# A tile of 64 bytes given up in a transformer layer on one core: the pools behind it begin 64 bytes lower

## The chip, the core and the metric

The kernel runs on one core of a Trainium2 chip. The metric is the device time of one execution in microseconds (us). TensorE (PE in the profile) multiplies: a matmul streams one operand from the on-chip memory SBUF against weights that a separate instruction (LDWEIGHTS, engine PEld) has loaded from SBUF. VectorE (DVE), ScalarE (ACT) and GpSimd (POOL) do the element-wise work, and SyncE (SP) and POOL issue the DMAs. SBUF has 128 partitions; an address below is a byte offset within a partition.

## What is computed

One layer of a bidirectional encoder, 1024 tokens by 1024 channels, in float32. Cut to what matters:

```python
mod = silu(c) @ w_ada + b_ada                 # sh1, sc1, gt1, sh2, sc2, gt2
h = rmsnorm(x, norm1_g) * (1 + sc1) + sh1
u, v, q, k, va, gate_a, gate_b = split(h @ w_in)
a_out = gmlp_branch(u, v, ...) @ w_a          # chunks of 128 positions
b_out = window_attention_branch(q, k, va, ...) @ w_b   # |t-s| <= 128, ALiBi, sink
merged = sigmoid(gate_a) * a_out + sigmoid(gate_b) * b_out
x = x + gt1 * (merged @ w_o)
h2 = rmsnorm(x, norm2_g) * (1 + sc2) + sh2
f_gate, f_up = split(h2 @ w_ffn_in)           # 2816 columns each
x = x + gt2 * ((silu(f_gate) * f_up) @ w_ffn_out)
```

## The kernel before

**Precision.** Each float32 operand is split into a high part rounded to the fast matmul type and a low rest (`A.copy` and a subtraction on DVE: `unit` L223, `split` L411, `split2` L1254). A product of two operands is three matmuls: high by high, high by low, low by high (`mm3` L231, `multiply` L1378). So the matmuls come in triples.

**Stages.** `half(0)` and `half(1)` (L643, called at L1780) do the input projection, the gMLP branch and the attention for 512 tokens each, up to about 390 us. `gate_products` (L1387) does the gates' projection and the merge for the remaining channels, `out_products` (L1491) the output projection, the second norm and the first steps of what follows. Then comes the feed-forward input projection with 22 column tiles (L2049 to L2123), from about 590 us, and the down projection (L2125 to L2250), from about 1014 us. From the gate products on, each 2x2 block product is done with seven block products instead of eight, after Strassen and Winograd: the list `STEPS` (L1374) names for each of the seven the weight unit, the streamed block and the PSUM bank. A step of the feed-forward (one column tile) is therefore 7 products of 12 matmuls with 512 columns: 4 row blocks by one triple. The order in a step is B11, B21, T2, T1, T3, B22, T4. The blocks B11 and B21 are tiles `h`; T3 and T4 are tiles of the pool mid; T1, T2 and B22 are tiles `tt1`, `tt2`, `b22` of the pool ffn (`fpt` L1248; the names in the profile are those of the tile, so a block T2 of the feed-forward appears as `b22h`, `b22l` and its B22 as `tt2h`, `tt2l`, L1792 and L1972). The weights are tiles `wh` and `wl`. Two weight units of the feed-forward lie in the ffn tile `first` (L1676). In the down projection (77 steps of 12 matmuls) `split_step` (L2040) puts three of five units into `wh` and `wl` and two of five into tiles `oh` and `ol` of the pool outp; there each unit holds both the weights and the streamed block.

**Order of the work.** In `out_products` a planner (`Plan`, L41) sorts the work of the engines by cost and due time; behind it the order is written out by hand. TensorE runs its queue in program order, and loads of units are issued one step and more ahead of their use.

**Where the tiles lie.** The pools are laid out one behind another: const, wpool, hpool, mid, t2, small (L156 to L161), and behind small whatever is open: apool and attp during `half` (L323), then ffn (`open_ffn` L573), then outp (L2126). Each buffer takes a multiple of 32 bytes. In the program before, the places are these:

| Pool | first tile at byte | remainder by 256 |
|---|---|---|
| const (`ident`, `zeros`, `identr`) | 16512 | 128 |
| wpool (`raw`, `wh`, `wl`) | 19776 | 64 |
| hpool (`h`) | 56640 | 64 |
| mid | 89408 | 64 |
| small | 171328 | 64 |
| `ngt1` in small | 175296 | 192 |
| `ngt` in small, 4 buffers | 175360 | 0 |
| apool, later ffn, later outp | 175488 | 128 |
| attp (`pt`, `vt`, `lb`) | 198848 | 192 |

All tiles of wpool, hpool, mid, ffn and outp have sizes that are multiples of 2048, so every one of them has the remainder of its pool. `kbuf` in apool is at 188608, remainder 192.

**The tile of the change.** `out_products` needs the gate of the output projection negated: eight numbers per partition, written once (L1501) and used as the scalar of `accumulate` (L1607) for the products whose sign is turned. Before, it is the tile `ngt1` of 16 numbers with one buffer. The down projection has a tile with the same use for four numbers of the second gate, `sm(4, "ngt")` (L2191), written at L2235 and read in `second_row` (L2184); `sm` (L193) makes a tile of pool small with the pool's four buffers.

Of the kernel before, what the change touches and what calls it, by code (L numbers as in the profile page):

```python
# [8 lines left out]
F32 = mybir.dt.float32  # L9
# [7 lines left out]
P = 128  # L17
D = 1024
S = 1024
KT = D // P  # L20
# [87 lines left out]
def kernel(  # L108
# [52 lines left out]
    small = ctx.enter_context(pool("small", 4))  # L161
# [5 lines left out]
    def nm(s):  # L167
        n_names[0] += 1
        return f"{s}_{n_names[0]}"
# [13 lines left out]
    def midt(dt, shape):  # L183
        return mid.tile([P, 2048], dt, tag="mid", name=nm("mid")).rearrange(
            "p (a b) -> p a b", a=shape
        )
# [6 lines left out]
    def sm(n, name):  # L193
        return small.tile([P, n], F32, tag=name, name=nm(name))
# [1296 lines left out]
    def out_products(merged):  # L1491
# [5 lines left out]
        B22 = oblk["B22"] = (fpt("b22h"), fpt("b22l"))  # L1497
        T3 = oblk["T3"] = (midt(F32R, 4), midt(F32R, 4))
        T4 = oblk["T4"] = (midt(F32R, 4), midt(F32R, 4))
        ngt = small.tile([P, 16], F32, tag="ngt1", name="ngt1", bufs=1)  # L1500
        V.tensor_scalar(ngt[:, :KT], mod[:, GT1 : GT1 + KT], -1.0, None, op0=ALU.mult)  # L1501
        gt = mod[:, GT1 : GT1 + KT]

# [280 lines left out]
    with tc.manual_schedule():  # L1784
        out_products(merged)
# [263 lines left out]
    with tc.manual_schedule():  # L2049
# [141 lines left out]
        ngt = sm(4, "ngt")  # L2191
# [130 lines left out]
```

## Time and profile before

| | us |
|---|---|
| median of 3 runs | 1229.14 (1228.86 to 1229.53) |
| the profiled execution, its time | 1231.04 |
| its span, first to last instruction | 1229.2 |
| TensorE busy in the span | 1217.7 |
| VectorE busy | 928.8 |
| ScalarE busy | 582.5 |

A row of a group of instructions gives the line (L145 is the helper that records every instruction, so tiles tell more than lines), engine, operation, the tiles as out<-in, shape, count, and then busy time and mean duration, or minimum/median/maximum. Matmuls overlap: the next one starts before the modelled end of the one before, so the distance between starts is the cost of one, and a longer duration shows a longer distance. In the chain of waits in order of time a row is start, length, what ran, and how many instructions; matmuls that end in one `mm` or `at` bank group stand in one row.

### The profile page before, as it was taken

What the parts mean: (1) busy time and instruction counts of PE and PEld (TensorE: products, weight loads), DVE (VectorE), ACT (ScalarE), POOL (GpSimd) and SP (SyncE); (2) the same over time, 40 slices, a digit from 0 to 9 for tenths busy, and PEclk for the clock granted to TensorE, in tenths of its full rate; (3) what the DMA queues carried; (4) which work ended last, traced back from release to release, by engine and by line L of the source; (5) the groups of instructions that cost most, each with busy time, mean ns of one, the idle gap of its engine ahead of it and who ended that gap; (6) DMA issues with size and microseconds to landing.
All of it is one profiled execution on the core that took longest, in us unless ns stands there. A gap on an engine that the chain in (4) does not pass through costs nothing.

```text
span 1229.2 us, 15626 instructions
## 1 busy us (share of the span) xinstructions
PE 1217.7 (99%) x5653; PEld 1007.4 (82%) x5653; DVE 928.8 (76%) x1504; ACT 582.5 (47%) x954; POOL 150.8 (12%) x182
## 2 busy tenths in 40 slices
PE   9999999999999999999999999999999999999998
PEld 7888888888788888878778888888888888888887
DVE  8999977789978776898897667575676766765646
ACT  5667855367855543645453333333333334433341
POOL 0024323024322000011000001010000000000001
PEclk9999999999999999999999999999999999999999
DMA  9743169644277333467313446455555449995552
GB/s 362 275 184 100 35 225 357 240 183 160 104 257 239 97 120 103 145 231 240 130 42 121 171 156 221 171 189 187 188 188 191 167 153 369 394 352 189 188 171 103
DMA packets 78097, 236.54 MB, mean 192 GB/s; under 512 B 8899, under 2 KB 9155, under 8 KB 72773
## 3 DMA queue, kind: packets, MB, share of 16 engines
q1 hardware_dynamic: 63028, 163.20, 38.3%
q0 software_dynamic: 14992, 72.36, 15.6%
q8 instruction: 44, 0.72, 0.2%
q14 instruction: 33, 0.26, 0.1%
HBM read 176.28 MB, written 59.24 MB: 192 GB/s over the span
## 4 chain that ended last, share of the span: by engine, by line
PE 92%; DVE 4%; DMA 2%; ACT 1%; issue 1%; SPq 0%; DVEq 0%; ACTq 0%
PE at L145 47%; PE mm L145 46%; DVE mid L145 1%; DMA raw<-in_w_q_dram 1%; DMA raw<-in_w_ada_dram 1%; DVE wl L145 1%; DVE t L145 0%; DMA mid<-in_xA_dram 0%; DVE wo L145 0%; DVE raw L145 0%; DVE pL L145 0%; ACT wh L145 0%; ACT mid L145 0%; DVE ss L145 0%; DVE tt1l L145 0%
## 5 line engine op out<-in xcount | busy, mean ns | idle before, releaser
L145 ACT CAST wh<-raw 128x1024 fp32r<-128x1024 f32 (+1 forms) x149 | 152.0, 1022 | 112.0 <-PE mm L145 33.4
L145 DVE TENSOR_TENSOR wl<-raw,wh 128x1024 fp32r<-128x1024 f32 (+1 forms) x135 | 158.9, 1181 | 60.4 <-ACT wh L145 59.9
L145 PE MATMUL mm<-mid,wh 128*128 128x512 f32 x640 | 198.9, 392 | 0.8 <-DVE mid L145 0.8
L145 PEld LDWEIGHTS mm<-mid,wh 128*128 128x128 f32 x640 | 119.8, 188 | 26.9 <-DVE mid L145 1.2
L145 PE MATMUL mm<-mid,wl 128*128 128x512 f32 x320 | 125.3, 392 | 0.0
L145 PE MATMUL mm<-wh,h 128*128 128x512 f32 x384 | 124.7, 396 | 0.6 <-ACT h L145 0.6
L145 PE MATMUL at<-h,wh 128*128 128x512 f32 x304 | 94.1, 391 | 0.8 <-DVE t L145 0.8
L145 PE MATMUL mm<-h,wh 128*128 128x512 f32 x304 | 94.3, 391 | 0.0
L145 PEld LDWEIGHTS mm<-wh,h 128*128 128x128 f32 x384 | 70.8, 188 | 14.1 <-ACT h L145 1.0
L145 DVE TENSOR_TENSOR wl<-ws,wh 128x1024 fp32r<-128x1024 f32 (+1 forms) x54 | 60.7, 1124 | 24.8 <-ACT wh L145 24.7
L145 ACT CAST wh<-ws 128x1024 fp32r<-128x1024 f32 (+1 forms) x54 | 52.6, 973 | 43.8 <-DVE ws L145 35.6
L145 PEld LDWEIGHTS mm<-mid,wl 128*128 128x128 f32 x320 | 60.0, 188 | 13.7
L145 PE MATMUL mm<-wl,h 128*128 128x512 f32 x192 | 71.1, 391 | 0.0
L145 PEld LDWEIGHTS at<-h,wh 128*128 128x128 f32 x304 | 56.8, 188 | 13.2 <-DVE t L145 1.6
L145 PEld LDWEIGHTS mm<-h,wh 128*128 128x128 f32 x304 | 56.7, 188 | 11.6
L145 ACT ACTIVATE t<-t 128x512 f32<-128x512 f32 x46 | 28.4, 630 | 71.6 <-DVE t L145 71.5
L145 DVE TENSOR_TENSOR ol<-raw,oh 128x1024 fp32r<-128x1024 f32 x30 | 36.6, 1224 | 31.9 <-ACT oh L145 30.4
L145 PE MATMUL mm<-h,wl 128*128 128x512 f32 x152 | 59.3, 390 | 0.0
L145 PE MATMUL at<-h,wl 128*128 128x512 f32 x152 | 59.2, 389 | 0.0
L145 ACT ACTIVATE xs<-xs 128x512 f32<-128x512 f32 x21 | 13.3, 632 | 96.2 <-DVE xs L145 96.2
L145 ACT CAST oh<-raw 128x1024 fp32r<-128x1024 f32 x30 | 31.6, 1054 | 45.3 <-PE at L145 23.6
L145 PE MATMUL at<-wl,wh 128*128 128x512 f32 (+1 forms) x136 | 52.8, 388 | 0.0
(296 smaller groups left out, 2885.7 us busy)
## 6 DMA issues: line engine op xcount, KB each, us to landing
mid<-in_w_ada_dram SPq DMA_DIRECT2D x28, 512.0 KB, 8.6
raw<-in_w_gate_dram SPq DMA_DIRECT2D x28, 512.0 KB, 3.8
tA<-hid POOLq DMA_DIRECT2D x11, 1024.0 KB, 4.3
tB<-hid POOLq DMA_DIRECT2D x11, 1024.0 KB, 5.0
wo<-in_w_out_dram POOLq DMA_DIRECT2D x22, 512.0 KB, 6.1
wS<-wo POOLq DMA_DIRECT2D x11, 1024.0 KB, 5.3
raw<-wS SPq DMA_DIRECT2D x44, 256.0 KB, 3.2
raw<-tB SPq DMA_DIRECT2D x44, 256.0 KB, 5.2
```

The costliest lines, as they stand in the source:

```text
L145: ins = f(*args, **kw)
```

## The change

The negated gate becomes a tile of the tag `ngt`, which has four buffers already. The tag's buffers are 32 bytes each afterwards (eight numbers); before, 16 bytes that took 32. The tile `ngt1` of 64 bytes is gone, so what lies behind pool small begins at 175424 instead of 175488. No instruction is added or removed.

```diff
-        ngt = small.tile([P, 16], F32, tag="ngt1", name="ngt1", bufs=1)
+        ngt = sm(KT, "ngt")
         V.tensor_scalar(ngt[:, :KT], mod[:, GT1 : GT1 + KT], -1.0, None, op0=ALU.mult)
         gt = mod[:, GT1 : GT1 + KT]
```

## Prediction

> **What bounds the kernel.** I read the page first, then the chain of waits in order of time, then the matmul groups by tile, then the timeline inside one feed-forward step.
>
> ```profile
> span 1229.2 us, 15626 instructions
> PE 1217.7 (99%) x5653; PEld 1007.4 (82%) x5653; DVE 928.8 (76%) x1504; ACT 582.5 (47%) x954; POOL 150.8 (12%) x182
> PE 92%; DVE 4%; DMA 2%; ACT 1%; issue 1%; SPq 0%; DVEq 0%; ACTq 0%
> ```
>
> TensorE is busy for 99% of the span, and 92% of the chain that ends last is TensorE. A change that adds and removes no instruction can only show if it changes what one matmul costs, or how often TensorE starves. The table by stretches says that starving is not the question behind 640 us:
>
> ```profile
> core 0: us, PE busy (x) PEld busy (x) DVE busy (x) ACT busy (x) POOL busy (x), PEclk, DMA share, GB/s
> 640.00:1020.00 380.00, 380.00 (x1658) 310.89 (x1657) 259.39 (x359) 130.05 (x178) 29.34 (x55) 1.00 0.49 174
> ```
>
> The clock granted is 1.00, DVE is busy for 259 of 380 us, and 1658 matmuls fill the 380 us: 229.2 ns from start to start. Is that what a 512-column matmul costs here? The chain in order of time (start, length, what, how many) says no:
>
> ```profile
> 153.00 5.44 PE mm L145 x24
> ...
> 347.22 46.27 PE mm L145 x204
> 407.25 5.49 PE mm L145 x24
> 426.50 5.49 PE mm L145 x24
> ...
> 534.55 30.40 PE mm L145 x132
> ...
> 569.86 16.49 PE mm L145 x72
> ...
> 706.59 38.51 PE at L145 x168
> ...
> 1014.74 60.05 PE at L145 x264
> 1074.79 60.09 PE mm L145 x264
> ```
>
> Where it goes best, 24 matmuls take 5.44 us (226.7 ns each), and 204 in a row keep that (46.27 / 204 = 226.8). Elsewhere, with no wait shown, the same shape takes 229.2 (38.51 / 168) and 227.5 (60.05 / 264). Which matmuls are the dear ones? By tile (duration min/median/max; the modelled end lies after the next start, so only differences count: 389 belongs to a spacing of 227, 394 to 232):
>
> ```profile
> L145 PE MATMUL at<-h,wh x304: 387/389/497, 393.3 to 1000.3; 128*128 128x512 f32 x152
> L145 PE MATMUL mm<-h,first x24: 390/395/398, 611.3 to 619.7; 128*128 128x512 f32 x24
> L145 PE MATMUL at<-h,first x24: 392/395/504, 614.2 to 623.3; 128*128 128x512 f32 x24
> ```
> ```profile
> L145 PE MATMUL at<-tt1h,wh x112: 388/394/478, 398.8 to 1005.6; 128*128 128x512 f32 x112
> L145 PE MATMUL at<-tt1h,wl x112: 392/392/397, 399.3 to 1006.0; 128*128 128x512 f32 x112
> L145 PE MATMUL at<-tt1l,wh x112: 387/388/397, 399.0 to 1005.8; 128*128 128x512 f32 x112
> ```
>
> The products that stream `h` are at the floor. Those that stream `tt1` (a tile of the pool ffn) are 394, 392, 388 in each triple of three: 5 + 3 - 1 = 7 ns over three floors of 389. `first` is `h` against weights in the same pool, and costs 6 more. The timeline of one step shows it in starts:
>
> ```profile
> 764.28 0.61 PE L145 MATMUL mm<-h,wh 128*128 128x512 f32 x2
> ...
> 769.73 0.40 PE L145 MATMUL mm<-b22h,wh 128*128 128x512 f32 x1
> ...
> 775.24 0.40 PE L145 MATMUL mm<-mid,wh 128*128 128x512 f32 x1
> ```
>
> Two products (24 matmuls) on `h` take 769.73 - 764.28 = 5.45 us, two on `b22` and `tt1` take 5.51. What the dear tiles have in common is where they lie. Added up from the pools in the code, the tiles of wpool, hpool and mid all start 64 bytes above a multiple of 256, and those of ffn and outp, behind the 4160 bytes of pool small, 128 above one. The dear matmuls are those in which the streamed tile and the weights differ in this (`tt1`, `tt2`, `b22` against `wh`; `h` against `first`), and about a dozen behind each change from one to the other: the 24 of 407.25 and 426.50 are a product on mid right behind one on ffn and one on `h`, 0.05 us above 5.44.
>
> **The change, part by part.** It adds and removes no instruction. The rows of the tile `ngt`:
>
> ```profile
> L145 DVE SCALAR_TENSOR_TENSOR mid<-mm,ngt,mid x12: 737/749/751, 538.8 to 580.9; 128x512 f32<-128x512 f32 x12
> L145 DVE SCALAR_TENSOR_TENSOR mid<-mid,ngt,mid x8: 743/746/747, 1208.2 to 1215.6; 128x512 f32<-128x512 f32 x8
> L145 DVE TENSOR_SCALAR ngt<-mod x2: 169/170/172, 143.2 to 1091.0; 128x8 f32<-128x8 f32 x1, 128x4 f32<-128x4 f32 x1
> ```
>
> (1) **The slot.** The gate is written once (0.17 us) and read twelve times until 580.9; the other `ngt` is written at 1091.0. The tag has four buffers for these two tiles, so no wait arises: 0. If the second had to wait for the first's readers, it would wait for something that ended 510 us earlier: still 0.
>
> (2) **The address.** ngt1 took 64 bytes. The tag ngt had four buffers of 16 bytes, each in a 32-byte slot, and has four of 32 now: 0 more. Pool small shrinks from 4160 to 4096 bytes, and apool, attp, ffn and outp begin 64 lower, so ffn and outp go from 128 to 64 above a multiple of 256, like all other matmul tiles from the gate products on; attp goes from 192 to 128. With a floor of 226.7 the terms are:
> - Feed-forward: a step has 7 products, 84 matmuls. 38.51 us for 168 is 0.43 above 168 x 0.2267 = 38.08, 0.21 for a step; 22 steps give 4.7.
> - Gate products: the starts 407.25 and 426.50 are 84 matmuls apart, 19.25 against 19.04: 0.21, six times: 1.3.
> - Output projection: 30.40 - 132 x 0.2267 = 0.48 and 16.49 - 72 x 0.2267 = 0.17: 0.65.
> - `first`: 48 matmuls by 395 - 389 = 6 ns: 0.3.
> - Down projection, where two of five weight units lie in outp: 264 matmuls are 59.85 at the floor and take 60.05 and 60.09, 0.22 above; 924 matmuls give 3.5 times this, 0.8.
>
> The sum is 7.7. All of it lies on the path, as TensorE has no idle time there. A little will stay (behind the row sums and spreads, which work on tiles of const, and at the stage borders): I take 7.4.
>
> (3) **Attention**, the first 385 us, is not cleaned: there attp goes from 192 to 128 while its partners stay at 64, and the tiles of const at 128.
>
> ```profile
> L145 PE MATMUL at<-kbuf,mid x128: 274/337/409, 78.9 to 321.3; 128*128 128x384 f32 x96, 128*128 128x256 f32 x32
> ```
>
> No row shows these tiles at 128. The bounds: 128 score products and, by the code, 88 products with `vt` (22 key blocks, two heads, two parts), 216 in all, each getting dearer by 9 ns (the widest step from median to maximum in the `tt1` rows, 388 to 397) is +1.9; each getting cheaper by the 5 ns of `tt1h` against `h` is -1.1. Score products stay between unlike tiles, as now, so I take 0 and keep both ends.
>
> (4) **Other engines.** The subtractions into a tile at 64 and into one at 128:
>
> ```profile
> L145 DVE TENSOR_TENSOR wl<-raw,wh 128x1024 fp32r<-128x1024 f32 x125 | 152.1, 1220 | 54.4 <-ACT wh L145 53.9
> ...
> L145 DVE TENSOR_TENSOR ol<-raw,oh 128x1024 fp32r<-128x1024 f32 x30 | 36.6, 1224 | 31.9 <-ACT oh L145 30.4
> ```
>
> 1220 and 1224 ns: DVE doesn't tell the places apart, 0. DMAs of equal size into the two places land so:
>
> ```profile
> ws<-in_w_up_dram SPq DMA_DIRECT2D x11, 512.0 KB, 5.7
> ru<-in_w_up_dram SPq DMA_DIRECT2D x11, 512.0 KB, 3.5
> ```
>
> `ru` moves to the residue of `ws`. At worst its loads take 2.2 us longer; by the code each is issued over one step (19.25 us between the starts 407.25 and 426.50) ahead of its use, and what it could delay is DVE, idle for 120 of those 380 us. I take 0.
>
> So 1229.14 - 7.4 = **1221.7**. The durations are those of the profiled execution, 1231.04 us with a span of 1229.2; it is 0.15% above the median, and the term is small enough to subtract it from the median as it is.
>
> **The rivals.** (a) *No difference, 1229.1.* The dear matmuls are dear for what they do, not for where they lie: all `tt` and `b22` products follow an eviction, or stream blocks just made. For it: no view shows an address. Against it: `first` holds weights, not a streamed block, and is dear too, while products on `h` with the same loop are at the floor. That the shift doesn't happen (a slot of 16 bytes that really grew to 32) ends here too. The Trainium skill, page "SBUF — State Buffer", section "Who interferes with whom", gives TensorE two independent read ports for streamed operand and weights and says "PE and ACT never wait on anyone"; by that rule the place of a tile can't matter and the time is this rival's. The trace disagrees so far: equal shapes, no wait, 389 against 394.
>
> (b) *Half.* Only the steady part goes (by the code 3 products of 12 matmuls in 22 + 6 + 4 steps, 1152 on ffn tiles, by 7/3 = 2.3 ns: 2.7 us, and the 0.3 of `first`), since transitions have another cause: 1229.14 - 3.0 = 1226.1. Against it: the transitions sit only behind ffn and outp tiles.
>
> (c) *Slower, by collision.* If streamed tile and weights hurt each other when they start on the same residue, all products on ffn now do so all the time. The price: every matmul on an ffn tile at the maximum of the `tt1` rows, 397, is 8 above the floor instead of 7/3, so 5.7 more in 1152: +6.5, 1235.6. It decides for slower as soon as equal residues cost more than those 2.3 ns. Against it: `h` and `wh` are at equal residues and at the floor.
>
> **How the numbers follow.** The forecast gets 0.78; its own range is 7.7 + 1.1 better, 1220.3, to 7.4 less 1.9, 1223.6. (b) gets 0.06, (a) 0.11, (c) 0.05. From 1220.0 to 1226.5 the range holds the forecast and (b), a little over 8 in 10. About 0.2% (2.5 us, so below 1226.7) is what a measurement of this kernel can tell from no change: faster 0.84, same 0.11, slower 0.05.
>
> **What would show it.** Right: 168 chained feed-forward matmuls in 38.1 us instead of 38.51; medians of `tt1h`, `b22h` and `first` at 389; the span of the first 385 us within 2 us. Wrong: `tt1h` still at 394 (a), mid products behind it still 0.05 above (b), `tt1` rows at 397 (c), or TensorE waits that weren't there, were something else nearly late.

## The result and the profile after

| | before | after |
|---|---|---|
| median, first comparison (5 runs each) | 1228.86 us (1227.65 to 1229.53) | 1223.76 us (1222.79 to 1225.07) |
| its ratio | | 0.9959 [0.9945, 0.9974] |
| median, later comparison (11 and 5 runs) | 1230.84 us (1228.22 to 1231.62) | 1223.26 us (1220.81 to 1224.36) |
| its ratio | | 0.9940 [0.9928, 0.9952] |
| span of the profiled execution of the first | 1229.2 us | 1223.2 us |

Faster, by 5.1 us in the first comparison and 7.6 in the later one, both ratios with their intervals below 1; 7.4 were forecast. Page of the kernel after: span, busy times, engines' shares of the chain of waits.

```profile
span 1223.2 us, 15626 instructions
PE 1212.0 (99%) x5653; PEld 1008.0 (82%) x5653; DVE 928.0 (76%) x1504; ACT 583.1 (48%) x954; POOL 150.6 (12%) x182
PE 94%; DVE 4%; issue 1%; DMA 1%; ACT 1%; SPq 0%; DVEq 0%; ACTq 0%
```

Nothing was taken out: the same 15626 instructions, the same 5653 matmuls, DVE, ACT and POOL as before within a us. TensorE alone is busy for 5.7 us less and is still the bound. The stretch from 640 to 1020 us (same columns as before):

```profile
640.00:1020.00 380.00, 380.00 (x1677) 314.38 (x1676) 261.84 (x359) 131.55 (x180) 29.34 (x55) 1.00 0.51 180
```

TensorE starts 1677 matmuls there in place of 1658, at the same clock: 226.6 ns each, the floor. The chain of waits of after in order of time:

```profile
346.92 46.28 PE mm L145 x204
...
406.79 5.44 PE mm L145 x24
425.83 5.44 PE mm L145 x24
...
533.26 30.26 PE mm L145 x132
...
704.71 38.08 PE at L145 x168
...
1009.57 59.84 PE at L145 x264
1069.41 59.84 PE mm L145 x264
1129.25 89.14 PE at L145 x396
```

The row of 204 is as it was. A pair on mid takes 5.44 us instead of 5.49, the 168 of the feed-forward 38.08 instead of 38.51, 264 of the down projection 59.84 instead of 60.05. By tile (min/median/max):

```profile
L145 PE MATMUL at<-tt1h,wh x112: 389/389/504, 398.5 to 1000.6; 128*128 128x512 f32 x112
L145 PE MATMUL at<-tt1h,wl x112: 387/389/396, 398.9 to 1001.0; 128*128 128x512 f32 x112
...
L145 PE MATMUL mm<-b22h,wh x72: 389/389/478, 567.9 to 997.8; 128*128 128x512 f32 x72
...
L145 PE MATMUL mm<-h,first x24: 388/389/389, 610.6 to 618.8; 128*128 128x512 f32 x24
L145 PE MATMUL at<-h,first x24: 387/391/504, 613.4 to 622.5; 128*128 128x512 f32 x24
```

394 and 392 have become 389, and the products on `first` went from 395 to 389 and 391 (the second half holds some that waited, hence its 504).

### The profile page after: what moved, and what is told of

Same layout as the page of the kernel before. It is cut to its first block, busy times and chain, and to the rows that moved or that the text cites. A ratio compares the mean times of both kernels' runs of the same rounds, so it can differ in the third digit from the quotient of the medians.

```text
span 1223.2 us, 15626 instructions
## 1 busy us (share of the span) xinstructions
PE 1212.0 (99%) x5653; PEld 1008.0 (82%) x5653; DVE 928.0 (76%) x1504; ACT 583.1 (48%) x954; POOL 150.6 (12%) x182
## 4 chain that ended last, share of the span: by engine, by line
PE 94%; DVE 4%; issue 1%; DMA 1%; ACT 1%; SPq 0%; DVEq 0%; ACTq 0%
PE mm L145 47%; PE at L145 47%; DVE mid L145 2%; DMA ws<-in_w_up_dram 1%; DVE wl L145 0%; DVE wo L145 0%; DVE ss L145 0%; DVE pL L145 0%; DVE ws L145 0%; ACT mid L145 0%; DVE h L145 0%; DVE t L145 0%; DVE tt1l L145 0%; ACT wh L145 0%; DVE lb L145 0%
## 5 line engine op out<-in xcount | busy, mean ns | idle before, releaser
L145 PE MATMUL at<-wh 128*128 128x512 f32 (+1 forms) x136 | 52.7, 388 | 0.0
```

The source lines that it names most:

```text
L145: ins = f(*args, **kw)
```

## The experiments

Theory P (place): a matmul is dear when the tile that it streams and the tile of its weights have different remainders by 256, and some matmuls behind each change of remainder are dear too. Its rivals: the slot of the small tile itself saves time; lower addresses, or a smaller pool, do; the dear matmuls are dear for what they do. All kernels compute the whole output; they only move tiles. Below, "remainder" is that by 256, and a row of 168 is the feed-forward's in the chain of waits.

**Four places for what lies behind pool small.** The kernel before, with its separate tile made longer:

```diff
-        ngt = small.tile([P, 16], F32, tag="ngt1", name="ngt1", bufs=1)
+        ngt = small.tile([P, N], F32, tag="ngt1", name="ngt1", bufs=1)   # N = 24, 32, 48, 64
```

N = 24 moves ffn and outp 32 bytes up, to remainder 160:

> The kernel before with its tile ngt1 enlarged from 64 to 96 bytes, so apool, attp, ffn and outp begin 32 bytes higher, at 175520, 160 above a multiple of 256. Theory (a triple is dear when streamed tile and weights start on unlike remainders, and clean when alike): 96 apart, unlike, so 168 chained feed-forward matmuls stay above the floor of 38.08 us, at 38.3 to 38.7, and the time stays within 3 us of before, 1226 to 1232. Rival (what counts is a start at a multiple of 64): much worse than before, over 39 us for 168. Rival (the gain comes from the slot, or from anything but the place): exactly as before, 38.51 and 1229.

N = 32, 64 bytes up, remainder 192:

> The kernel before with ngt1 enlarged to 128 bytes: the pools behind it begin at 175552, 192 above a multiple of 256, 128 away from the weights. Theory with remainders by 256: still unlike, 38.3 to 38.7 us for 168 feed-forward matmuls and 1226 to 1232 us. Theory with remainders by 128: 64 and 192 are alike, so 38.08 and about 1223.5. Rival (only the slot, or only a lower address): as before, 38.51 and 1229.

N = 48, 128 bytes up, remainder 0:

> The kernel before with ngt1 enlarged to 192 bytes: the pools behind it begin at 175616, remainder 0 by 256, 192 away from the weights. Theory with remainders by 256 or by 128: unlike, 38.3 to 38.7 us for 168 and 1226 to 1232 us. Rival (remainder by 64 alone): clean, but so would the kernel before be. Rival (absolute alignment to 256 is best): 38.08 or less and 1223 or less.

N = 64, 192 bytes up, remainder 64 like the change, but at a higher address and without the slot:

> The kernel before with ngt1 enlarged to 256 bytes: the pools behind it begin 192 bytes higher, at 175680, with the remainder 64 that they have in the changed kernel. Nothing of the slot is used. Theory: as the changed kernel, 38.08 us for 168 feed-forward matmuls, 59.84 for 264 of the down projection, 1223.8 us. Rival (the slot, or a lower address, makes the gain): as before, 38.51, 60.05 and 1229.

Measured beside the kernel before at 1230.56 us (1228.17 to 1231.67), with before and after for comparison:

| kernel | remainder of ffn and outp, less 64 | 168 of the feed-forward | 264 of the down projection | ratio to before |
|---|---|---|---|---|
| after | 0 | 38.08 | 59.84 | 0.9959 [0.9945, 0.9974] and 0.9940 [0.9928, 0.9952] |
| 192 up | 0 | 38.08 | 59.84 | 0.9953 [0.9939, 0.9967] |
| before | +64 | 38.51 | 60.05 | 1 |
| 32 up | +96 | 38.77 | 60.24 | 1.0035 [1.0023, 1.0047] |
| 64 up | +128 | 38.59 | 59.92 | 1.0002 [0.9993, 1.0011] |
| 128 up | 192, or -64 | 38.64 | 60.05 | 1.0019 [1.0009, 1.0028] |

The chain rows of 32 up, 64 up, 128 up and 192 up, one fence for each:

```profile
707.51 38.77 PE at L145 x168
...
1017.70 60.24 PE at L145 x264
```
```profile
707.44 38.59 PE at L145 x168
...
1016.13 59.92 PE at L145 x264
```
```profile
709.13 38.64 PE at L145 x168
...
1018.25 60.05 PE at L145 x264
```
```profile
702.79 38.08 PE at L145 x168
...
1007.43 59.84 PE at L145 x264
```

192 up gives the gain of the change (1224.45 us, 1222.56 to 1225.76) with a larger pool at higher addresses, so neither the slot nor a lower address is needed for it. 64 up shows that equal remainders by 128 are not enough: ffn at 192 and weights at 64 differ by 128, and the 168 stay dear; of the differences tried, only 0 by 256 is at the floor. The places are not all alike bad: +96 is worse than +64, and +64 cheaper than -64.

Two expectations were missed in their size. 32 up is dearer than said: 38.77 us where 38.3 to 38.7 were expected, and 1234.68 us (1233.18 to 1235.51), 4.1 above before where 3 were allowed. 128 up, at 1232.12 us (1230.38 to 1234.5), lies 0.12 beyond its range of 1226 to 1232. 64 up, at 1230.67 us (1229.17 to 1231.89), is as expected. Which places are dear came out as the theory says; how dear each of them is doesn't follow from it.

**The slot without the address.** The changed kernel, with 64 bytes given back in the tile `ss`, so that all behind pool small lies where it did before:

```diff
-        return small.tile([P, 640], F32, tag="ss", name=nm("ss"), bufs=1)
+        return small.tile([P, 656], F32, tag="ss", name=nm("ss"), bufs=1)
```

> The changed kernel with the tile ss of pool small enlarged by 64 bytes: the slot is used as in the change, but the pools behind small begin at 175488 again, remainder 128, as before. Theory (only the place counts): as before, 38.51 us for 168 feed-forward matmuls, 60.05 for 264 of the down projection, time within 0.2% of before. Rival (the slot counts): as the changed kernel, 38.08 and 0.4% below before.

1230.31 us (1228.14 to 1231.6) against 1231.0 (1229.51 to 1232.87): ratio 0.9993 [0.9984, 1.0002]. The chain row of the 168:

```profile
707.10 38.51 PE at L145 x168
```

With the slot and the old address the dear matmuls are back to the digit. The slot is worth nothing that can be measured.

**Another remainder for all.** The changed kernel with 64 bytes more in const, so that wpool, h, mid, ffn and outp all have remainder 128 (attention's own tiles 192):

```diff
-    nhalf = const.tile([P, 16], F32, tag="nhalf", name="nhalf")
+    nhalf = const.tile([P, 32], F32, tag="nhalf", name="nhalf")
```

> The changed kernel with one const tile enlarged by 64 bytes: wpool, hpool, mid, ffn and outp all begin at remainder 128, apart from nothing but the early part of const, which was at 128 already. Theory (streamed tile and weights must have like remainders, whichever): clean, 38.08 for 168, 59.84 for 264, 0.4% below before. Rival (the remainder 64 itself is the good one, or the lower address): dear as before or dearer, 38.5 and 1229.

1222.76 us (1220.48 to 1224.11) against 1231.0: 0.9930 [0.9918, 0.9943].

```profile
702.66 38.08 PE at L145 x168
```

The floor again. It is the difference that counts, not remainder 64; before, ffn at 128 was dear, here it is not.

**Only the weights moved.** The changed kernel with `wh` and `wl` 64 bytes up, at 128, and all else left at 64:

```diff
     crow = wpool.tile([P, UNIT], F32, tag="raw", name="crow")[:, :512]
+    wpad = wpool.tile([P, 16], F32, tag="wpad", name="wpad", bufs=1)
+    hpad = hpool.tile([P, 48], F32, tag="hpad", name="hpad", bufs=1)
```

> The changed kernel with only wh and wl moved to remainder 128 (64 bytes put ahead of them, 192 behind), everything else at 64. Then every product of the gates, the output projection and the feed-forward streams a tile at 64 against weights at 128, 192 away by 256, as the ffn products of the kernel that was moved up by 128 bytes, which cost 6.7 ns a matmul above the floor. Theory: some 2690 matmuls by 2.3 to 6.7 ns, so 6 to 18 us above the changed kernel, and 1 to 5 more in attention, 1231 to 1247; the products on h, clean in all kernels so far, turn dear (median above 389). In the down projection wh streams against wh and stays clean but for the changes to oh. Rival (only the place of the streamed tile counts): h, mid and ffn are where they are in the changed kernel, so 1224 and h at 389.

1242.83 us (1239.0 to 1243.49) against 1231.0: 1.0088 [1.0072, 1.0103], slower. Chain, then the products on `h`, which lie where they did:

```profile
347.61 47.60 PE mm L145 x204
...
713.06 39.20 PE at L145 x168
```
```profile
L145 PE MATMUL mm<-h,wh x304: 391/394/483, 122.9 to 1009.2; 128*128 128x512 f32 x152
...
L145 PE MATMUL at<-h,wh x304: 392/394/502, 395.1 to 1012.0; 128*128 128x512 f32 x152
...
L145 PE MATMUL mm<-h,first x24: 388/389/395, 616.7 to 624.9; 128*128 128x512 f32 x24
```

This is the clearest run: products on `h`, at the floor in before (389), go to 394 with their weights 64 bytes away, and 168 matmuls take 39.20 us, 6.7 ns dearer each ((39.20 - 38.08) / 168). It is the -64 of 128 up, now in all products of the feed-forward and of the gates; as all seven products of a step have the same difference, no change between neighbours is in these 6.7 ns. The products on `h` whose weights lie in `first`, which stayed at 64, keep the median 389 in the same profile. That a matmul is dear for what it does is refuted: same tiles, same order, no wait at these products, another place of the weights.

**Attention too.** The changed kernel with the tiles of const and of attention also at 64:

```diff
+    cpad = const.tile([P, 48], F32, tag="cpad", name="cpad")
     ident = const.tile([P, P], F32, tag="ident", name="ident")
...
-    nhalf = const.tile([P, 16], F32, tag="nhalf", name="nhalf")
+    nhalf = const.tile([P, 32], F32, tag="nhalf", name="nhalf")
...
-    nsink = apool.tile([P, NH], F32, tag="nsink", name="nsink")
+    nsink = apool.tile([P, NH + 48], F32, tag="nsink", name="nsink")[:, :NH]
```

> The changed kernel with the tiles of const, kbuf and attp moved to remainder 64 too, so that all operands of all matmuls begin alike. Theory: from 385 us on nothing changes (38.08, 59.84). In the first 385 us the matmuls are 1.9 us above the floor in the changed kernel, part of it where 256- and 384-column matmuls mix with 512-column ones, which this doesn't touch: 0 to 1.9 us less, 1222 to 1224 beside a changed kernel at 1223.8. Rival (attention's excess comes from mixed lengths alone): 1223.8, the same excess.

1223.85 us (1222.57 to 1224.25) against 1231.0: 0.9938 [0.9925, 0.9950]. The attention rows, of before, of after and of this kernel:

```profile
L145 PE MATMUL at<-pL,vt x44: 389/389/396, 92.7 to 336.6; 128*128 128x512 f32 x44
```
```profile
L145 PE MATMUL at<-kbuf,mid x128: 278/334/407, 77.5 to 319.3; 128*128 128x384 f32 x96, 128*128 128x256 f32 x32
...
L145 PE MATMUL at<-pL,vt x44: 390/394/397, 91.3 to 336.3; 128*128 128x512 f32 x44
```
```profile
L145 PE MATMUL at<-kbuf,mid x128: 274/338/411, 78.4 to 319.7; 128*128 128x384 f32 x96, 128*128 128x256 f32 x32
...
L145 PE MATMUL at<-pL,vt x44: 389/389/389, 92.2 to 335.1; 128*128 128x512 f32 x44
```

The 44 products on `pL` are cleaned by it (394 to 389, 0.2 us). By the code `pL` and its partner `vt` both lie in attp in every kernel, so what differs there is the neighbours: attp is 128 away from `wh` and `h` in before (389), 64 in after (394) and 0 here. The 128 score products are not cleaned: 338, as in before (337), with `kbuf` and `mid` both at 64. These mix 384 and 256 columns; what their spread comes from stays open, but it is not a difference of remainders. No gain of the kernel beyond the change's can be told.

**The best versions side by side, and one stage alone.** The changed kernel again, the two all-alike versions again, and the changed kernel with only outp (`oh`, `ol`) back at remainder 128:

```diff
         outp.append(ctx.enter_context(pool("outp", 9)))
+        outp[0].tile([P, 16], F32, tag="opad", name="opad", bufs=1)
```

> The changed kernel itself, beside the others of this call. Question: of the 7.2 us that the profile of after has less than before behind 385 us, the median showed 5.1. If the rest was a short stretch of half clock and a late load of the profiled execution, the profile without such a stretch has a span near 1221.5 and the median lies 6 to 7.5 us below before's, ratio 0.994 to 0.995. If the address change gives less than the sum of its steps, the ratio stays at 0.996, with 168 feed-forward matmuls at 38.08 us all the same.

> Streamed tiles and weights all at remainder 128 (attention's at 192), against the changed kernel at 64. If only the difference of the two remainders counts, the time is that of the changed kernel within 0.1% (ratio of the two 0.999 to 1.001), and 0.993 earlier was the luck of a chip and of a DMA arrival. If remainder 128 is better than 64 in itself, it is 3 us faster than the changed kernel on this chip too.

> Tiles of const and attention also at remainder 64. If only the difference counts and attention's excess of 1.9 us is not one of place: same time as the changed kernel within 0.1%. If attention had gained, up to 1.9 us less than the changed kernel.

> The changed kernel with the pool of the down projection's second weight tiles (oh, ol) 64 bytes up, at remainder 128 as before the change, all else as in the changed kernel. If the term of the down projection (0.8 us) is the place of these tiles alone: chain rows of 264 matmuls back at 60.05 to 60.09 us in place of 59.84, everything ahead of 1010 us as in the changed kernel (168 in 38.08), and a time 0.8 us above the changed kernel's, 0.07%. If the down projection's excess came from elsewhere (what the step does, or what ran ahead of it), the rows stay at 59.84.

| beside before at 1230.84 us (1228.22 to 1231.62) | us | ratio |
|---|---|---|
| after | 1223.26 (1220.81 to 1224.36) | 0.9940 [0.9928, 0.9952] |
| all at 128 | 1222.54 (1222.24 to 1224.73) | 0.9942 [0.9930, 0.9953] |
| all at 64, attention too | 1223.18 (1220.55 to 1225.43) | 0.9941 [0.9929, 0.9953] |
| outp at 128 | 1224.21 (1222.69 to 1225.35) | 0.9950 [0.9937, 0.9963] |

The first three cannot be told apart, so the 0.9930 of all at 128 above was no better version, and none beats the change. The chain and the products on `oh` of the fourth:

```profile
703.29 38.08 PE at L145 x168
...
1007.95 60.05 PE at L145 x264
1068.00 60.09 PE mm L145 x264
1128.10 89.47 PE at L145 x396
```
```profile
L145 PE MATMUL at<-oh x84: 389/389/397, 1015.9 to 1211.9; 128*128 128x512 f32 x84
```

60.05, 60.09 and 89.47 are the three rows of before, to the digit, while the feed-forward keeps its 38.08. The term of the down projection is the place of outp alone: 0.21 + 0.25 + 0.33 = 0.8 us; its time, 0.95 us above after's, agrees but lies within the intervals. This kernel also separates the two halves of theory P. In a product on `oh` streamed tile and weights have the same remainder, 128; what differs is the neighbour product at 64. So a change of remainder from one product to the next costs by itself (389/389/397 here, 389/389/389 in after). The cost sits in the matmuls behind the change. After one change from `wh` to `oh`, eleven matmuls take 2.54 us, where eleven at the floor are 2.49 (11 x 0.2267); these are the starts of the first and of the twelfth:

```profile
1043.25 0.39 PE L145 MATMUL at<-oh 128*128 128x512 f32 x1
...
1045.79 0.39 PE L145 MATMUL at<-oh,ol 128*128 128x512 f32 x1
```

**A rest that is not the change's.** The first profile of after lost time in two places. Its chain, and its stretch from 326 to 334 us, then the same of the profile of the changed kernel run again:

```profile
329.13 6.68 PE mm L145 x24
```
```profile
326.00:334.00 8.00, 6.87 (x25) 5.47 (x26) 7.82 (x20) 5.38 (x11) 3.20 (x3) 0.79 0.37 151
```
```profile
329.65 5.47 PE mm L145 x24
```
```profile
326.00:334.00 8.00, 6.58 (x31) 4.97 (x31) 7.78 (x19) 5.56 (x12) 2.46 (x3) 1.00 0.48 191
```

A mean granted clock of 0.79 over 8 us, and 24 matmuls in 6.68 us instead of 5.47: 1.2 us that the second profile of the same program doesn't have. The dip is not the change's: the profile of the slot alone, with the old address, has it at the same place, and that of 128 up too (0.79).

```profile
326.00:334.00 8.00, 6.59 (x24) 4.92 (x23) 7.78 (x20) 5.58 (x11) 2.75 (x3) 0.79 0.44 177
```

The other place is the first load of the feed-forward's weights. On it hangs a chain of VectorE steps up to the block `t` for which TensorE waits, here the chain of after, TensorE's wait in its timeline, and the chain of all at 64, run again:

```profile
591.38 7.14 DMA ws<-in_w_up_dram
```
```profile
602.01 0.73 PE L145 MATMUL at<-h,wh 128*128 128x512 f32 x2 [1.79 <-DVE t L145]
```
```profile
589.86 4.40 DMA ws<-in_w_up_dram
```

The same load took 7.14 us in one profile of the changed kernel, 5.70 in the other and 4.40 to 6.70 in the other kernels with equal remainders. In before the wait at this place was 0.81 us:

```profile
602.78 0.73 PE L145 MATMUL at<-h,wh 128*128 128x512 f32 x2 [0.81 <-DVE t L145]
```

So about 1.0 us of the gain turned into a longer wait in that one profile (1.79 - 0.81). In the kernel with the load of 4.40 us the timeline shows no wait there.

The second profile of the changed kernel has no dip and a wait of only 0.38 us at this place. Its span should then have been near 1221.5 us, and that was missed: it is 1222.5, 0.7 below the first's 1223.2. It lost time elsewhere, partly at a wait for a GpSimd step that the first profile doesn't show:

```profile
568.00 1.16 PE L145 MATMUL at<-ident,rcol 128*128 128x128 f32 x8 [0.97 <-POOL rcol L145]
```

So both executions have losses of about a us of their own. The dip and the late load are real losses of the first profile, but they don't explain why the first comparison shows less than the later one.

## Why the prediction was right

**The mechanism** held: no step of it failed, one term was sized too high. By its terms, from the rows of before and after:

| term | predicted, us | measured, us | from |
|---|---|---|---|
| feed-forward | 4.7 | 4.7 | 11 x (38.51 - 38.08) |
| gate products | 1.3 | 1.3 | 6 x (19.25 - 19.04), starts of 406.79 and 425.83 |
| output projection | 0.65 | 0.28 | 30.40 - 30.26 for the 132, 16.58 - 16.44 for the 72 |
| `first` | 0.3 | 0.24 | 24 x (395 - 389) + 24 x (395 - 391), in ns |
| down projection | 0.8 | 0.8 | rows of 264, 264, 396 |

The chain of after cuts the 72 up differently, so both numbers are from starts: of the first of these matmuls and of the one behind the last, in before, then in after:

```profile
569.61 0.48 PE L145 MATMUL mm<-b22h,wh 128*128 128x512 f32 x1
...
586.19 0.63 PE L145 MATMUL at<-h,wh 128*128 128x512 f32 x2
```
```profile
567.93 0.48 PE L145 MATMUL mm<-b22h,wh 128*128 128x512 f32 x1
...
584.37 0.61 PE L145 MATMUL at<-h,wh 128*128 128x512 f32 x2
```

The output projection was sized too high: the floor was taken for the whole row of 132, of which 30.26 - 132 x 0.2267 = 0.34 us stays in after too, at equal remainders. The terms sum to 7.3 us, where 7.7 were worked out and 7.4 taken. "All of it lies on the path, as TensorE has no idle time there" was a little too strong: behind the output projection TensorE waits for the block `t` (0.81 us in before), and this wait took 1.0 of the gain back in one profile and none in another.

**The size at the end.** The first comparison has 5.1 us, [3.2, 6.8] by its interval (1228.86 x 0.0026 to 0.0055). The median of after hardly differs in the two comparisons (1223.76 and 1223.26); that of before does (1228.86 there, 1230.56, 1231.0 and 1230.84 in the three others). The later comparison has 7.4 by its ratio, [5.9, 8.9]. Over the seven comparisons of kernels with equal remainders the mean ratio is 0.9943, 7.0 us of 1230.8. So 7.3 us of cheaper matmuls arrive at the end nearly whole; why before was 2 us faster in the one comparison stays open. The first time, 1223.76, is 2.1 us above the 1221.7 and 0.2 outside the forecast's own narrow range (1220.3 to 1223.6), though well inside the wide one. That the later comparison, with 7.6 by its medians, meets the 7.4 so closely is partly luck, as its interval shows.

**Step 1, the slot:** 0, as the run with the slot alone shows. **Step 2, the address:** the places are those worked out, and only the remainder matters, as 192 up shows. **Step 3, attention:** 0, inside the bounds, by two opposite changes: `pL` products went from 389 to 394 (44 x 5 ns = +0.2 us), score products from 337 to 334 (128 x 3 ns = -0.4; by medians of mixed shapes, so roughly). One reading behind its bounds was wrong: it set all partners of attp's tiles at 64, but by the code `pH`, `pL` and `vt` lie in attp together. **Step 4, DVE and DMA:** DVE busy is 928.0 against 928.8; no load of `ru` came onto the chain, and its loads, now on the remainder of `ws`, land in 3.7 us (3.5 before), not in the 5.7 of `ws`, as the view of the DMA issues of after has it (KB each, median us from issue to landing):

```profile
ru<-in_w_up_dram SPq DMA_DIRECT2D x11, 512.0 KB, 3.7
```

A load did come onto the chain, but it was the first of `ws`, whose time scatters between executions of one program.

**The rivals.** (a) No difference: refuted by 192 up, the slot alone and the weights moved. The Trainium skill, page "SBUF — State Buffer", section "Who interferes with whom", calls TensorE's read ports for the streamed operand and for the weights independent and is about engines that wait for each other. What the prediction drew from it, that the place of a tile can't matter, doesn't hold here: 389 against 394 for products on `h`, by the place of the weights alone. (b) Half, since transitions have another cause: refuted, the pairs on mid fell to 5.44 with the rest, and outp at 128 brings back the down projection's part by itself. (c) A collision at equal remainders: the opposite is true, equal remainders are the floor at 64 and at 128.

**What is only argued:** why the remainder matters. The runs show that the cost hangs on the difference of two start addresses by 256 and that weight loads run beside the stream (PEld is busy for 82% of the span). That the two reads of SBUF meet in some part of 256 bytes is a picture that fits, and no run here shows it.

## What to carry to other kernels

Where equal matmuls differ by a few ns and no wait is shown, group them by tile and put the start address of the streamed tile and of the weights beside each group; 64 bytes of a small tile somewhere in front may be the whole cause. In a kernel like this one (matmuls of 128x512, each with its own weights loaded beside the one before), keep all tiles that TensorE reads in a dense stage on one remainder by 256, and check it again after any edit to a small pool, since such an edit moves everything behind it (ratios to before from 0.993 to 1.009 among the placements tried here). When a change of 0.5% is judged, ask a second profile which of the stalls are the program's: the first one here has a clock dip and a late load, the second a late GpSimd step, about a us each, and the cheaper matmuls stand alike in both.

## What the runs showed that was not expected

- The cost of a difference is not symmetric and not monotone: with streamed tile less weights at +64, 168 matmuls with 3 of 7 products on such tiles are 0.43 us over the floor, at +96 0.69, at +128 0.51, at -64 0.56. With all seven products at -64 it is 1.12.
- These figures add up both halves of theory P, and the neighbours are nearly half. By the starts of the matmuls in the steady feed-forward steps of before, those on `h` are 226.7 ns apart on average, those on ffn tiles 228.9 to 230.3, and those on mid, which have the remainder of their weights but follow ffn tiles, 230.8. That is 24 x 4.1, some 100 of the 215 ns that a step lies over the floor. In 128 up and in the run with the weights moved the matmuls at -64 are 233.3 apart.
- The down projection, where only neighbours differ, orders them otherwise: 264 matmuls are 0.21 over the floor at +64, 0.40 at +96, 0.08 at +128 and 0.21 at -64. A change of remainder by 128 is nearly free, a difference of 128 within a product is not.
- The granted clock fell to a mean of 0.79 over the 8 us from 326 us in the profiles of three kernels (after, the slot alone, 128 up) and stayed at 1.00 there in others, the second of the changed kernel among them. A wait of TensorE of about 1.4 us near 327 us stands ahead of it in after (1.40), but also in before (1.39) and in the second profile (1.43), which have no dip; what decides stays open.
